# Loading through both DMA queues at the start of an RMSNorm-GELU kernel

## Chip, cores, metric

One core of one Trainium2 chip. The metric is the device time of one execution in microseconds (us). Runs of the kernel before spread by 0.3 to 0.9 us within a job; medians and extremes are given where a difference is that small.

## The reference

x is 8 x 1024 x 2048 float32 (67.1 MB), and so is the result:

```python
rms = np.sqrt(np.mean(x ** 2, axis=-1, keepdims=True) + eps)
out = gamma * x / rms
return 0.5 * out * (1 + np.tanh(np.sqrt(2 / np.pi) * (out + 0.044715 * out ** 3)))
```

## The kernel before

The 8192 rows are 16 groups of 512 rows: 128 partitions with 4 rows (32,768 contiguous bytes) each, 4 MB a group. Six slots hold groups in on-chip memory, and a slot is loaded again when its group has been stored. ScalarE sums squares, GpSimd makes the reciprocal root, VectorE multiplies by gamma (spread over the partitions by four matmuls into PSUM), and ScalarE does GELU with the root as its scale. SyncE issues the loads (queue q1). ScalarE issues gamma's loads and the stores (queue q10).

```python
P, ROWS, SLOTS, GW, CHUNK, NARROW = 128, 4, 6, 32, 512, 128
# ... (pools, tiles: slot[6] is [128, 4, 2048]; gamma_row is [1, D // GW, GW + 4])
    store_pieces = {
        0: [(R, [(0, NARROW), (NARROW, R * D)])],          # group 0: a 64 KB piece first
        G - 1: [(1, [(r * D, r * D + D)]) for r in range(R)],
    }
    def load(g):
        nc.sync.dma_start(out=slot[g % SLOTS], in_=x3[g])
# ... (squares, scale, inverse_rms, gelu_store: whole groups; the last one row by row)
    with tc.manual_schedule():
        for k in range(0, D, CHUNK):                       # gamma: four pieces
            nc.scalar.dma_start(
                out=gamma_row[:, k // GW : (k + CHUNK) // GW, 0:GW],
                in_=gamma[k : k + CHUNK].rearrange("(o a b) -> o a b", o=1, b=GW),
            )
        for g in range(SLOTS):
            load(g)
# ... (constants, four matmuls)
        for g in range(G + 1):
            if g < G:
                squares(g); inverse_rms(g); scale(g)
            if g:
                gelu_store(g - 1)
                if g - 1 + SLOTS < G:
                    load(g - 1 + SLOTS)
```

## Time and profile before

| | before |
|---|---|
| time, median of 3 | 317.31 us (317.09 to 317.42) |
| span of the profiled execution | 315.5 us |
| bytes moved by DMA | 134.25 MB |
| rate from 50 to 270 us | 433 GB/s |

The span is about 1.8 us less than the time. The rate row matters most: the DMA engines are at one fixed rate nearly all the time, so the kernel's length is bytes over rate, plus the places where the engines do less. The lines that show this stand in the prediction.

The trace records each DMA packet; a packet here is one partition's contiguous run. A 32,768-byte one takes 1.213 us at full rate, and the large ones are nearly in proportion (8,192 bytes: 0.309 us for 0.303). **Stall** means what packets of over 4,000 bytes took beyond that (less 12 ns for each, so that rounding is left out), summed over the packets that start in a stretch of time and divided by the 16 engines. The records don't name a packet's engine, so a stall is a mean over the engines.

### The profile page before, as it was taken

The page shows a single profiled execution, that of the slowest core. Times are in us where ns is not written, and L with a number is a line of the kernel's source. Part 1 is how long each engine was busy: PE and PEld are TensorE (multiplying, and loading weights), DVE is VectorE, ACT ScalarE, POOL GpSimd, SP SyncE. Part 2 cuts the span into 40 slices and gives each one's busy share as a digit, 9 for nine tenths or more (in the row PEclk, how much of TensorE's full clock was granted, in tenths as well). Part 3 has the DMA queues.
Part 4 walks back from the last instruction along what each step waited for, and adds up shares of the span by engine and source line. Part 5 has one row for each costly group of instructions (what it writes and reads, how often), then busy time and mean ns, then how long its engine had stood idle before and what let it go on. Part 6 is the DMA issues. An engine that isn't in the chain of part 4 may idle for free.

```text
span 315.5 us, 479 instructions
## 1 busy us (share of the span) xinstructions
PE 7.9 (3%) x8; PEld 2.1 (1%) x8; DVE 139.4 (44%) x21; ACT 251.2 (80%) x194; POOL 32.3 (10%) x101
## 2 busy tenths in 40 slices
PE   0810000000000000000000000000000000000000
PEld 0200000000000000000000000000000000000000
DVE  0028909091918282827328082370824609480000
ACT  1289999999999999989596895969959599598500
POOL 0020202020202020202020020200202002020000
DMA  8999999999999999999999999999999999999997
GB/s 329 404 461 403 459 413 396 453 406 462 403 461 407 457 407 458 411 453 416 449 428 440 432 432 432 432 440 424 446 416 453 411 453 411 453 415 449 416 418 314
DMA packets 5315, 134.25 MB, mean 426 GB/s; under 512 B 704, under 2 KB 832, under 8 KB 832
## 3 DMA queue, kind: packets, MB, share of 16 engines
q1 hardware_dynamic: 2304, 67.11, 49.7%
q10 hardware_dynamic: 3008, 67.12, 49.4%
q14 instruction: 3, 0.02, 0.0%
HBM read 67.12 MB, written 67.11 MB: 425 GB/s over the span
## 4 chain that ended last, share of the span: by engine, by line
ACT 38%; DMA 32%; another core or an unknown queue 18%; issue 5%; ACTq 1%; SPq 0%
ACT slot L111 21%; DMA slot<-in_x_dram 16%; ACT junk L73 16%; DMA out_dram<-slot 15%; ACTq L119 1%; SPq L69 0%; ACTq L111 0%; ACTq L73 0%
## 5 line engine op out<-in xcount | busy, mean ns | idle before, releaser
L83 DVE TENSOR_TENSOR slot<-slot,gamma_ps 128x8192 f32<-128x8192 f32 (+1 forms) x19 | 139.2, 7338 | 142.3 <-ACT junk L73 142.3
L73 ACT ACTIVATE junk<-slot 128x2048 f32<-128x2048 f32 x64 | 120.4, 1881 | 40.8 <-DMA slot<-in_x_dram 36.8
L111 ACT ACTIVATE slot<-slot,rstd 128x2048 f32<-128x2048 f32 x64 | 123.0, 1987 | 1.7 <-ACT slot L111 1.7
L93 POOL TENSOR_SCALAR ms<-ssq 128x4 f32<-128x4 f32 x16 | 3.1, 194 | 242.8 <-ACT junk L73 242.8
L97 POOL TENSOR_TENSOR y<-ms,power 128x4 f32<-128x4 f32 x16 | 16.1, 1009 | 1.3
L73 ACT ACTIVATION_READ_ACCUMULATOR junk<-slot 128x1 f32 x64 | 11.9, 186 | 0.0
L134 PE MATMUL gamma_ps<-gamma_row,ones 1*128 1x512 f32 x8 | 7.9, 1112 | 9.2 <-DMA gamma_row<-in_gamma_dram 9.2
L132 ACT ACT_TABLE_LOAD x1 | 1.3, 1283 | 3.3 <-issue 3.3
L99 POOL TENSOR_TENSOR z<-z,ms 128x4 f32<-128x4 f32 x16 | 3.2, 201 | 1.3
L103 POOL TENSOR_TENSOR rstd<-z,y 128x4 f32<-128x4 f32 x16 | 3.2, 200 | 1.3
L98 POOL TENSOR_TENSOR z<-y 128x4 f32<-128x4 f32 x16 | 3.2, 200 | 1.3
L100 POOL TENSOR_SCALAR z<-z 128x4 f32<-128x4 f32 x16 | 3.1, 195 | 1.4
L134 PEld LDWEIGHTS gamma_ps<-gamma_row,ones 1*128 1x128 f32 x8 | 2.1, 306 | 13.4 <-issue 8.7
L130 DVE MEMSET warm<- 1x1 f32 x1 | 0.1, 59 | 0.8 <-PEq L166 0.8
L132 ACT ACTIVATE warm<-warm 1x1 f32<-1x1 f32 x1 | 0.2, 203 | 0.0
L131 DVE MEMSET ones<- 1x128 f32 x1 | 0.2, 165 | 0.0
L129 POOL MEMSET power<- 128x4 f32 x1 | 0.1, 102 | 0.3 <-POOLq L166 0.3
L166 POOL MEMSET const-float32-0.0<- 128x1 f32 x1 | 0.1, 99 | 0.2 <-issue 0.2
L166 POOL MEMSET const-bfloat16-1.0<- 128x1 bf16 x1 | 0.1, 102 | 0.0
L166 POOL MEMSET const-uint8-127<- 128x1 uint8 x1 | 0.1, 102 | 0.0
L166 POOL MEMSET const-float32-1.0<- 128x1 f32 x1 | 0.1, 99 | 0.0
## 6 DMA issues: line engine op xcount, KB each, us to landing
slot<-in_x_dram SPq DMA_DIRECT2D x16, 4096.0 KB, 29.9
out_dram<-slot ACTq DMA_DIRECT2D x14, 4096.0 KB, 43.3
out_dram<-slot ACTq DMA_DIRECT2D x4, 1024.0 KB, 17.5
out_dram<-slot ACTq DMA_DIRECT2D x1, 4032.0 KB, 28.5
gamma_row<-in_gamma_dram ACTq DMA_DIRECT2D x4, 2.0 KB, 10.3
out_dram<-slot ACTq DMA_DIRECT2D x1, 64.0 KB, 14.4
```

What stands on the lines that cost most here:

```text
L73: nc.scalar.activation(out=junk, in_=slot[g % SLOTS][:, r, :], func=ACT.Square, accum_out=ssq[:, g, r : r + 1],)
L83: nc.vector.tensor_tensor(out=rows, in0=rows, in1=gamma_ps.unsqueeze(1).to_broadcast([P, n, D]), op=ALU.mult,)
L93: v.tensor_scalar(out=ms, in0=ssq[:, g, :], scalar1=1.0 / D, scalar2=eps_f, op0=ALU.mult, op1=ALU.add,)
L97: v.tensor_tensor(out=y, in0=ms, in1=power, op=ALU.pow)
L98: v.tensor_tensor(out=z, in0=y, in1=y, op=ALU.mult)
L99: v.tensor_tensor(out=z, in0=z, in1=ms, op=ALU.mult)
L100: v.tensor_scalar(out=z, in0=z, scalar1=-0.5, scalar2=1.5, op0=ALU.mult, op1=ALU.add)
L103: v.tensor_tensor(out=rstd[:, g, :], in0=z, in1=y, op=ALU.mult)
L111: nc.scalar.activation(out=slot[g % SLOTS][:, r, :], in_=slot[g % SLOTS][:, r, :], func=ACT.Gelu_apprx_tanh, scale=rstd[:, g, r : r + 1],)
L119: nc.scalar.dma_start(out=dst[:, a:b], in_=flat[:, a:b])
L132: nc.scalar.activation(out=warm, in_=warm, func=ACT.Gelu_apprx_tanh)
L134: nc.tensor.matmul(out=gamma_ps[:, k : k + CHUNK], lhsT=ones, rhs=gamma_row[:, k // GW : (k + CHUNK) // GW, 0:GW], start=True, stop=True,)
```

## The change

Its intent: let both queues load at first, so that loads are through early, and let ScalarE's queue pass from its last load to its first store without a gap, so that the small first store piece is not needed.

```diff
-GW = 32
-CHUNK = 512
-NARROW = 128
+HALF = 2
+GW = 64
+GAMMA = [(0, 1024), (1024, 1536), (1536, 2048)]
...
-    gamma_row = sbuf.tile([1, D // GW, GW + 4], FP32, name="gamma_row")
+    gamma_row = sbuf.tile([1, D // GW, GW + 8], FP32, name="gamma_row")
...   (load, store, squares, scale, gelu take a range of rows now; no small store piece)
+        load(nc.sync, 0, 0, HALF)
+        for a, b in GAMMA:
+            nc.scalar.dma_start(
+                out=gamma_row[:, a // GW : b // GW, 0:GW],
+                in_=gamma[a:b].rearrange("(o a b) -> o a b", o=1, b=GW),
+            )
-        for g in range(SLOTS):
-            load(g)
+        load(nc.scalar, 0, HALF, R - HALF)
+        load(nc.sync, 1)
+        load(nc.scalar, 2)
+        load(nc.scalar, 3, 0, 1)
+        load(nc.sync, 3, 1, R - 1)
+        load(nc.sync, 4)
+        load(nc.sync, 5)
...
+        squares(0, 0, HALF)
+        for g in range(G):
+            squares(g, HALF, R - HALF)
+            inverse_rms(g)
+            step = 1 if g in (0, G - 1) else HALF
+            for r in range(0, R, step):
+                scale(g, r, step)
+            if 0 < g < G - 1:
+                squares(g + 1, 0, HALF)
+            if g < G - 1:
+                gelu(g, 0, R)
+                store(g)
+                if g == 0:
+                    squares(1, 0, HALF)
+            else:                      # last group: gelu and store row by row, as before
...
+            if g + SLOTS < G:
+                load(nc.sync, g + SLOTS)
```

More of the change, by code (lines that the diff above doesn't have):

```diff
@@ L58, with load, store, squares @@
     junk = psum.tile([P, D], FP32, name="junk")
-    whole = [(R, [(0, R * D)])]
-    store_pieces = {
-        0: [(R, [(0, NARROW), (NARROW, R * D)])],
-        G - 1: [(1, [(r * D, r * D + D)]) for r in range(R)],
-    }
-    scale_pieces = {G - 1: [(0, 1), (1, 1), (2, 1), (3, 1)]}
-    def load(g):
-        nc.sync.dma_start(out=slot[g % SLOTS], in_=x3[g])
-    def squares(g):
-        for r in range(R):
+    def load(queue, g, r=0, n=R):
+        queue.dma_start(
+            out=slot[g % SLOTS][:, r : r + n, :], in_=x3[g, :, r : r + n, :]
+        )
+    def store(g, r=0, n=R):
+        nc.scalar.dma_start(
+            out=o3[g, :, r : r + n, :], in_=slot[g % SLOTS][:, r : r + n, :]
+        )
+    def squares(g, r, n):
+        for q in range(r, r + n):
             nc.scalar.activation(
                 out=junk,
-                in_=slot[g % SLOTS][:, r, :],
+                in_=slot[g % SLOTS][:, q, :],
                 func=ACT.Square,
-                accum_out=ssq[:, g, r : r + 1],
+                accum_out=ssq[:, g, q : q + 1],
             )
-    def scale(g):
-        for r, n in scale_pieces.get(g, [(0, R)]):
-            rows = slot[g % SLOTS][:, r : r + n, :]
-            nc.vector.tensor_tensor(
-                out=rows,
-                in0=rows,
-                in1=gamma_ps.unsqueeze(1).to_broadcast([P, n, D]),
-                op=ALU.mult,
-            )
+    def scale(g, r, n):
+        rows = slot[g % SLOTS][:, r : r + n, :]
+        nc.vector.tensor_tensor(
+            out=rows,
+            in0=rows,
+            in1=gamma_ps.unsqueeze(1).to_broadcast([P, n, D]),
+            op=ALU.mult,
+        )
     def inverse_rms(g):
@@ L103, in inverse_rms, with gelu @@
         v.tensor_tensor(out=rstd[:, g, :], in0=z, in1=y, op=ALU.mult)
-    def gelu_store(g):
-        flat = slot[g % SLOTS].rearrange("p r d -> p (r d)")
-        dst = o3[g].rearrange("p r d -> p (r d)")
-        row = 0
-        for n, stores in store_pieces.get(g, whole):
-            for r in range(row, row + n):
-                nc.scalar.activation(
-                    out=slot[g % SLOTS][:, r, :],
-                    in_=slot[g % SLOTS][:, r, :],
-                    func=ACT.Gelu_apprx_tanh,
-                    scale=rstd[:, g, r : r + 1],
-                )
-            row += n
-            for a, b in stores:
-                nc.scalar.dma_start(out=dst[:, a:b], in_=flat[:, a:b])
+    def gelu(g, r, n):
+        for q in range(r, r + n):
+            nc.scalar.activation(
+                out=slot[g % SLOTS][:, q, :],
+                in_=slot[g % SLOTS][:, q, :],
+                func=ACT.Gelu_apprx_tanh,
+                scale=rstd[:, g, q : q + 1],
+            )
     with tc.manual_schedule():
-        for k in range(0, D, CHUNK):
+        load(nc.sync, 0, 0, HALF)
+        for a, b in GAMMA:
             nc.scalar.dma_start(
-                out=gamma_row[:, k // GW : (k + CHUNK) // GW, 0:GW],
-                in_=gamma[k : k + CHUNK].rearrange("(o a b) -> o a b", o=1, b=GW),
-            )
-        for g in range(SLOTS):
-            load(g)
+                out=gamma_row[:, a // GW : b // GW, 0:GW],
+                in_=gamma[a:b].rearrange("(o a b) -> o a b", o=1, b=GW),
+            )
+        load(nc.scalar, 0, HALF, R - HALF)
[5 more added lines that the diff above has]
+        load(nc.sync, 5)
         nc.gpsimd.memset(power, -0.5)
@@ L132 @@
         nc.scalar.activation(out=warm, in_=warm, func=ACT.Gelu_apprx_tanh)
-        for k in range(0, D, CHUNK):
+        for k in range(0, D, 512):
             nc.tensor.matmul(
-                out=gamma_ps[:, k : k + CHUNK],
+                out=gamma_ps[:, k : k + 512],
                 lhsT=ones,
-                rhs=gamma_row[:, k // GW : (k + CHUNK) // GW, 0:GW],
+                rhs=gamma_row[:, k // GW : (k + 512) // GW, 0:GW],
                 start=True,
@@ L140 @@
             )
-        for g in range(G + 1):
-            if g < G:
-                squares(g)
-                inverse_rms(g)
-                scale(g)
-            if g:
-                gelu_store(g - 1)
-                if g - 1 + SLOTS < G:
-                    load(g - 1 + SLOTS)
+        squares(0, 0, HALF)
[13 more added lines that the diff above has]
+            else:
+                for r in range(R):
+                    gelu(g, r, 1)
+                    store(g, r, 1)
+            if g + SLOTS < G:
+                load(nc.sync, g + SLOTS)
 _INS = ['x', 'gamma', 'eps']
```

## The prediction

> **What bounds the kernel now.** I read the page's summary first, then stretches of time with their DMA rate, then the waits of the load queue, then the packet records of the two DMA queues.
>
> ```profile
> span 315.5 us, 479 instructions
> PE 7.9 (3%) x8; PEld 2.1 (1%) x8; DVE 139.4 (44%) x21; ACT 251.2 (80%) x194; POOL 32.3 (10%) x101
> DMA  8999999999999999999999999999999999999997
> q1 hardware_dynamic: 2304, 67.11, 49.7%
> q10 hardware_dynamic: 3008, 67.12, 49.4%
> HBM read 67.12 MB, written 67.11 MB: 425 GB/s over the span
> ```
>
> ScalarE, the busiest engine, is idle for a fifth of the span. The DMA row is at nine tenths in all slices but the first and last, and the two queues (q1: SyncE's loads; q10: ScalarE's stores and gamma) take 99.1% of the 16 engines' time. The chain that ended last names ScalarE first (38%), but it runs along an engine that itself waits for loads, in 10 of the 16 groups:
>
> ```profile
> ACT junk L73 <- DMA slot<-in_x_dram: 36.8, 10, 8.7
> ```
> ```profile
> SPq L69 <- DMA out_dram<-slot: 224.3, 10, 53.7
> ```
>
> ScalarE waits 36.8 us for loads; the load queue waits 224.3 us for stores that free a slot. Both are waits on the same DMA engines. The question is therefore only where those engines run below their rate:
>
> ```profile
> 0.00:4.00 4.00, 0.00 (x0) 0.00 (x0) 0.22 (x2) 0.73 (x1) 0.29 (x5) 1.00 0.73 238
> 4.00:44.00 40.00, 7.89 (x8) 2.10 (x8) 17.37 (x2) 29.14 (x27) 4.01 (x12) 1.00 1.00 429
> 44.00:50.00 6.00, 0.00 (x0) 0.00 (x0) 2.71 (x1) 5.97 (x6) 2.00 (x6) 1.00 1.02 393
> 50.00:270.00 220.00, 0.00 (x0) 0.00 (x0) 110.22 (x13) 191.76 (x147) 23.98 (x72) 1.00 1.00 433
> 304.00:315.50 11.50, 0.00 (x0) 0.00 (x0) 0.00 (x0) 0.00 (x0) 0.00 (x0) 1.00 0.82 348
> ```
>
> Last column GB/s. It is 433 over the 220 us in the middle, whatever the mix of loads and stores, and lower in three places: the start, 44 to 50 us, and the last slice. (A packet is counted where it starts, so a short stretch is rough.)
>
> The packet records say it per engine. A full load packet is one partition's 32,768 bytes and takes 1.213 us; the 134.22 MB of x and out are 256 such packets for each of 16 engines, 310.5 us. The first packets start at 1.73 to 2.61 us. Summing what 32,768-byte packets took over 1.213 us, per engine, I find 0.71 us in the first packet, 0.68 us between 44 and 52 us, and under 0.09 us in all the rest. The last packet ends at 314.3: about 2.1 for the start, 310.5, 0.7, 0.7, and some 0.3 for small packets. So of the span only about 5 us is not full-rate transfer. This bounds any gain of a change that moves the same bytes.
>
> The stretch at 44 to 50 us is where the first store begins: a 64 KB piece (128 columns) issued at 33.1 us, whose packets alternate with loads, then the other 4,032 KB, whose first packet starts at 46.76 us. From the moment the small piece's completion is written (45.12 us on the first engine) load packets take 1.4 to 2.0 us. When the next store follows on a running store queue (completions at 65.2 to 67.0 us), every packet takes 1.213 us. The stall is thus a cost of starting the store stream once, not of each store.
>
> **The Trainium skill.** "DMA: Bandwidth & Descriptors", section "Issuing engines are not separate DMA queues", says that transfers started from different engines run on the same 16 DMA engines and interleave, so that a second issuer saves only issue time. The trace agrees: q1 alone moves 433 GB/s at 16 to 34 us, q1 and q10 together 433 later. Section "Where 436 GB/s comes from" gives 435 GB/s as the ceiling of the on-chip fabric; 433 is measured, so two loading queues have no bandwidth to win. Section "Queues, rings and completion order" says that an engine takes turns between its queues packet by packet. The trace agrees: while the 512-byte store packets ran, each followed one 1.213 us load packet. That rule I use below to place the loads.
>
> **The change, part by part.**
>
> *Bytes and small packets.* The same 134.22 MB. A 512-byte packet took 27 ns where the full rate gives 19, so a packet costs some 8 ns beyond its bytes. Group 0 in halves adds 8 packets per engine, group 3 in two parts 8, the small store's removal takes 8 away, gamma goes from four pieces to three: under +0.1 us, and I enter +0.05.
>
> *Order of loads (estimate by taking turns).* SyncE's half of group 0 (16 KB packets) starts as before near 1.7 us. ScalarE issues three gamma pieces first, 0.61 us each in the trace, then its half. Before, the first gamma packet started only at 6.10 us, after four load packets per engine; those are now half as long, so gamma and then the half come in from about 5 to 10 us. SyncE's half lands near 8 us; the other half then alternates with group 1's 32 KB packets (0.61 + 1.21 us, eight times, 14.6 us) and lands at 20 to 24 us, as does group 1. Before, all of group 0 landed at 13.4 and group 1 at 23.0. Group 2 and three quarters of group 3 alternate next ((1.21 + 0.91) x 8 = 17 us, to about 41), then group 3's single row beside group 4 ((0.30 + 1.21) x 8 = 12 us, to about 53).
>
> *First store.* After the second half at 20 to 24: two squares (2.03 us each), 2.3 for the chain on POOL (one row of it in the trace: 21.66 to 24.07), four GELUs of 1.91: store 0 is issued at 34 to 39 us. VectorE's row pieces (2.28 us each in the old last group) mostly lie beside this. Before it was 38.8. At that time ScalarE's queue still holds loads until about 53, so store 0 does follow them directly. Store 1 is ready some 20 us later (59), store 0 lands near 72: from here ScalarE (about 16 us a group) stays ahead of the engines (8.39 MB at 433, 19.4 us a group).
>
> *What it removes from the path.* If the stall belongs to starting a queue, or to the small piece's completion, it goes: -0.68 us. The earlier gamma and the finer pieces on ScalarE and VectorE are beside the transfers and worth nothing. The start stays: the first packet of SyncE is issued at the same moment. Issue time saved: none on the path.
>
> *Slack at the end.* Before:
>
> ```profile
> 271.61 1.88 ACT L73 ACTIVATE junk<-slot 128x2048 f32<-128x2048 f32 x1 [3.68 <-DMA slot<-in_x_dram]
> ...
> 295.02 2.00 ACT L111 ACTIVATE slot<-slot,rstd 128x2048 f32<-128x2048 f32 x1 [0.42 <-ACT slot L111]
> 297.05 0.34 ACTq L119 DMA_DIRECT2D out_dram<-slot  x1
> ```
>
> The last load's data are used at 271.6, the last row is issued at 297.1, and the stores drain until 314.3: 17 us of backlog, of which one 1 MB row needs 2.4. After, the last load is issued when store 9 lands. Stores land 19.4 us apart from about 72, so near 246; it finds its queue nearly empty and needs 20 to 22 us. The landing, about 267, is no later than before, and the new order adds only about 2 us behind it (two squares come ahead of group 14's GELUs). The backlog stays over 10 us: the end is still set by transfers.
>
> Sum: 317.31 + 0.05 - 0.68 = 316.7 if the stall goes, 317.4 if it stays. I give the first 0.65: 316.9; I set 316.8, as an end some tenths lower is possible if the first stall overlaps the second queue's.
>
> **The rivals.** *The stall is that of the first writes to HBM, not of the queue.* Then it moves to about 53 us and the time is 317.4. For it: reads began with a stall of the same size (0.71), and 512-byte writes had been trickling too thinly to count. Against it: those writes ran from 36 us and did not slow a load, and the slow packets begin at that piece's completion. *The stall grows without the small piece in front,* which looks like an earlier cure: up to 0.7 more, 318.0. *ScalarE's half of group 0 comes so late that store 0 misses the end of the loads.* It would have to be 14 us later than I worked out; SyncE's queue would still hold group 5, so even then only the stall returns, 317.4. *The end becomes compute:* the last load would have to land after about 280; then each further us counts. Nothing speaks for it but the early delay of group 0. *Two loading queues move more:* against the measured 433 with one and with two, no.
>
> **Range and chances.** The two main outcomes are 316.7 and 317.4; runs of the old kernel spread by 0.33 us; the start stall may move by some tenths with 16 KB packets. So 316.2 to 317.7. Two per cent is 6.3 us, more than all time not at full rate (about 5 us), so faster by 2% has 0.01. Slower by 2% needs a compute-bound end or idle queues that nothing above shows: 0.02.
>
> **What would show it.** Right: rate 433 from about 5 us to the end with no dip near 53; store 0 issued at 34 to 39, long before its first packet; group 0's second half in at 20 to 24 us; last store issued at 290 to 300. Wrong: a dip where the first store starts (rival 1 or 2), a load queue and a store queue both empty in the middle, or the final stretch with DMA idle before the last row.

## The result, and the profile after

| | before | after |
|---|---|---|
| time, median of 4 each | 317.28 us (317.09 to 317.42) | 318.11 us (317.86 to 318.32) |
| ratio of fast runs, 95% interval | | 1.0026 (1.0009 to 1.0043) |
| span of the profiled execution | 315.5 us | 316.5 us |
| stall in the first packets (0 to 10 us) | 0.69 us | 0.73 us |
| stall where the first store begins | 0.66 us, at 45 to 49 us | 0.71 us, at 48 to 53 us |
| stall after that, to 284 us | 0.04 us | 0.82 us, nearly all at 84 to 88 us |
| the last store's 16 completions | 313.6 to 314.6 us | 314.0 to 315.7 us |

A ratio is the mean time of one kernel's fast runs over that of the other's of the same rounds, so it is not quite the ratio of the medians. The change is within 2%, and it is slower by about 0.8 us. In this job no run of one kernel overlaps one of the other; in the next they do (a_repeat below).

The page of the changed kernel, with the rows that answer to those of before:

```profile
span 316.5 us, 524 instructions
PE 7.2 (2%) x8; PEld 2.5 (1%) x8; DVE 141.0 (45%) x38; ACT 251.3 (79%) x194; POOL 32.1 (10%) x101
DMA  8999999999999999999999999999999999999997
q10 hardware_dynamic: 3232, 74.46, 54.6%
q1 hardware_dynamic: 2160, 59.77, 44.5%
HBM read 67.12 MB, written 67.11 MB: 424 GB/s over the span
```

The work of the engines is the same, and the DMA row has no hole. 7.3 MB of loads have moved from q1 to q10. The waits (who, for whom; us in total, times, longest), first ScalarE's and then the load queue's:

```profile
ACT junk L73 <- DMA slot<-in_x_dram: 27.6, 7, 10.5
```
```profile
SPq L62 <- DMA out_dram<-slot: 229.7, 10, 61.9
```

ScalarE waits 9 us less for loads than before (27.6 against 36.8), and the end comes later all the same: these waits were not what bounded the kernel. The rate by stretches, changed kernel first, then the same late stretch before:

```profile
4.00:48.00 44.00, 7.16 (x8) 2.48 (x8) 14.31 (x6) 26.45 (x23) 3.13 (x8) 1.00 1.01 433
48.00:54.00 6.00, 0.00 (x0) 0.00 (x0) 6.00 (x2) 5.97 (x6) 0.86 (x5) 1.00 0.98 369
54.00:84.00 30.00, 0.00 (x0) 0.00 (x0) 15.58 (x5) 28.97 (x24) 3.98 (x12) 1.00 1.01 436
84.00:90.00 6.00, 0.00 (x0) 0.00 (x0) 3.67 (x1) 6.00 (x4) 0.00 (x0) 1.00 1.01 382
90.00:270.00 180.00, 0.00 (x0) 0.00 (x0) 88.93 (x21) 160.31 (x125) 20.79 (x62) 1.00 1.00 433
```
```profile
84.00:90.00 6.00, 0.00 (x0) 0.00 (x0) 4.15 (x1) 5.55 (x5) 0.00 (x0) 1.00 1.01 437
```

The last column shows two dips where there was one: 369 GB/s where the first store begins, and 382 at 84 to 90 us, where the kernel before had 437. The column before it, the DMA share, stays near 1 in both dips: the engines count as busy, but single load packets take up to 2.6 us in place of 1.213. A busy share does not show this; the rate does.

The end was not bound by compute. In order of time on ScalarE, the last row:

```profile
298.04 2.00 ACT L106 ACTIVATE slot<-slot,rstd 128x2048 f32<-128x2048 f32 x1 [0.42 <-ACT slot L106]
300.07 0.34 ACTq L67 DMA_DIRECT2D out_dram<-slot  x1
```

The last store is issued at 300.07 us and the stores drain until 315.7.

The two profiled executions differ by 1.08 us (318.32 and 317.24); their last packets end at 315.38 and 314.30. The mean of the last store's 16 completions moved by 0.99 us (313.90 to 314.89). The new dip accounts for about 0.8 of this, the other two stalls for under 0.1. The slowest engine now ends 1.7 us after the first, in place of 1.0, but against the mean it lost only 0.1.

### The profile page after: what moved, and what is told of

Read it like the earlier page. It is cut to its first block, busy times and chain, and to the rows that moved or that the text cites. A ratio compares the mean times of both kernels' runs of the same rounds, so it can differ in the third digit from the quotient of the medians.

```text
span 316.5 us, 524 instructions
## 1 busy us (share of the span) xinstructions
PE 7.2 (2%) x8; PEld 2.5 (1%) x8; DVE 141.0 (45%) x38; ACT 251.3 (79%) x194; POOL 32.1 (10%) x101
## 3 DMA queue, kind: packets, MB, share of 16 engines
q10 hardware_dynamic: 3232, 74.46, 54.6%
## 4 chain that ended last, share of the span: by engine, by line
ACT 31%; DMA 30%; another core or an unknown queue 18%; issue 12%; ACTq 2%; POOL 1%; SPq 0%; POOLq 0%
ACT slot L106 20%; DMA slot<-in_x_dram 15%; DMA out_dram<-slot 15%; ACT junk L73 11%; ACTq L67 1%; ACTq L116 1%; POOL y L96 1%; SPq L62 0%; POOL z L98 0%; POOL z L97 0%; POOL ms L92 0%; POOL z L99 0%; POOLq L189 0%; POOL rstd L102 0%
## 5 line engine op out<-in xcount | busy, mean ns | idle before, releaser
L82 DVE TENSOR_TENSOR slot<-slot,gamma_ps 128x4096 f32<-128x4096 f32 (+1 forms) x36 | 140.8, 3944 | 148.9 <-ACT junk L73 135.6
L73 ACT ACTIVATE junk<-slot 128x2048 f32<-128x2048 f32 x64 | 120.4, 1881 | 35.2 <-DMA slot<-in_x_dram 27.6
L132 PE MATMUL gamma_ps<-gamma_row,ones 1*128 1x512 f32 x8 | 7.2, 1072 | 7.0 <-DMA gamma_row<-in_gamma_dram 7.0
## 6 DMA issues: line engine op xcount, KB each, us to landing
slot<-in_x_dram SPq DMA_DIRECT2D x13, 4096.0 KB, 27.6
```

Source lines behind the costliest of these rows:

```text
L73: nc.scalar.activation(out=junk, in_=slot[g % SLOTS][:, q, :], func=ACT.Square, accum_out=ssq[:, g, q : q + 1],)
L82: nc.vector.tensor_tensor(out=rows, in0=rows, in1=gamma_ps.unsqueeze(1).to_broadcast([P, n, D]), op=ALU.mult,)
L132: nc.tensor.matmul(out=gamma_ps[:, k : k + 512], lhsT=ones, rhs=gamma_row[:, k // GW : (k + 512) // GW, 0:GW], start=True, stop=True,)
```

## Experiments

Names that begin with a_ are edits of the changed kernel, b_ of the kernel before. Each job timed the kernel before on the same chip: its medians were 317.33 to 317.55. The jobs ran on different chips (the first three on one, the fourth and the fifth on two others), and the unedited changed kernel ran in the first alone, besides the run of the result, so kernels of different jobs are compared by their ratio to the kernel before. "Later stall" is what comes after the stall at the first store, up to 284 us.

| run | time, us | at the first store | later stall | last store's completions |
|---|---|---|---|---|
| a_repeat | 318.05 (317.57 to 318.13) | 0.71 | 0.38 | 313.7 to 314.9 |
| a_reversed | 318.21 (318.02 to 318.43) | 0.68 | 0.92 | 314.2 to 315.5 |
| b_no_small | 317.44 (317.14 to 317.55) | 0.61 | 0.13 | 313.5 to 314.9 |
| a_g3_sync | 323.51 (322.60 to 324.51) | 0.78 | 3.41 | 314.5 to 320.2 |
| a_halves | 323.03 (321.95 to 323.60) | 0.83 | 2.28 | 314.8 to 319.7 |
| a_small | 317.78 (317.16 to 318.33) | 0.53 | 0.51 | 313.8 to 315.0 |
| a_loads_sync | 322.67 (322.56 to 323.07) | 0.94 | 0.06 | 319.7 to 319.9 |
| b_load_gap | 320.92 (318.82 to 321.74) | 0.65 | 4.03 | 317.0 to 319.0 |
| a_half_row | 318.12 (317.83 to 318.30) | 0.86 | 0.37 | 313.7 to 315.7 |
| b_two_queues | 317.46 (317.34 to 317.59) | 0.48 | 0.11 | 313.3 to 314.8 |
| a_gamma_even | 317.22 (317.19 to 317.72) | 0.59 | 0.07 | 313.6 to 314.7 |
| b_two_queues_g8 | 317.51 (317.16 to 317.81) | 1.00 | 0.04 | 313.8 to 314.9 |
| a_even_plus8 | 318.70 (317.81 to 321.32) | 0.67 | 0.97 | 313.7 to 316.7 |
| a_even_plus16 | 317.81 (317.61 to 317.99) | 0.67 | 0.20 | 313.6 to 314.8 |
| a_gamma_even2 | 317.40 (317.19 to 317.69) | 0.49 | 0.07 | 313.4 to 314.6 |
| a_early_store | 317.56 (317.35 to 317.66) | 0.50 | 0.07 | 313.7 to 314.6 |

All outputs are right.

### First job: does it repeat, and what does it follow?

**a_repeat**: no edit.

> The changed kernel once more, for a second profile of it. If the two stalls of its load packets (0.71 us per engine at 48 to 52 us, 0.73 us at 84 to 88 us, over 1.213 us a packet) belong to the program, both come again within 2 us of the same place and the time is 318.0 +- 0.3. If the second was an accident of that one profiled execution, it is gone from this profile, and the other runs' times (all 0.6 us or more above the kernel before) need another cause.

Both stalls came again at the same places. The second was smaller (0.30 us at 84 to 90 us), and this profiled execution was the fastest of its four, 317.57. So the second dip belongs to the program, but its size varies from one execution to the next. The ratio to the kernel before was 1.0014 (0.9999 to 1.0029): this job alone does not show the changed kernel to be slower.

**b_no_small**, one line out of the kernel before:

```diff
-        0: [(R, [(0, NARROW), (NARROW, R * D)])],
```

> The kernel before without the small first piece of store 0 (one 4 MB store as for the other groups). Theory A (the stall at 45 to 49 us is that of starting bulk stores, whatever goes ahead): still one stall of about 0.7 us, starting when store 0's first packets start (some 5 us after its issue, so at 42 to 46 us); time 317.0 to 317.5. Theory B (the small piece is what the changed kernel lacks, and its absence costs the second stall): a second stall of about 0.7 us later on, time 317.8 to 318.2.

One stall of 0.61 us, at 40 to 43 us, where the whole store 0 now starts; time as before. Theory B falls for this kernel: the small piece neither keeps a stall away nor costs anything.

**a_g3_sync**:

```diff
-        load(nc.scalar, 3, 0, 1)
-        load(nc.sync, 3, 1, R - 1)
+        load(nc.sync, 3)
```

> The changed kernel with all of group 3 on SyncE's queue, so that the queue still has loads left when store 0 lands. Theory C (the second stall follows from the load queue running empty at 72 us and starting again at 76): the queue does not run empty, the second stall is gone, one stall of 0.7 us stays, time 317.2 to 317.6. Theory B (absence of the small piece) or D (address): two stalls remain, time about 318.

Neither theory had this. The load queue did not run empty and the dip at 84 us went, but from 68 us on store packets were slow all along, 3.0 us per engine in sum. Stretches of this kernel:

```profile
50.00:68.00 18.00, 0.00 (x0) 0.00 (x0) 10.91 (x4) 17.48 (x15) 1.99 (x6) 1.00 1.01 437
68.00:90.00 22.00, 0.00 (x0) 0.00 (x0) 12.55 (x3) 21.49 (x16) 2.00 (x6) 1.00 0.99 416
90.00:270.00 180.00, 0.00 (x0) 0.00 (x0) 87.82 (x20) 153.14 (x120) 19.95 (x60) 1.00 1.01 426
```

426 GB/s over 180 us in place of 433, by moving 1 MB of one load to the other queue. Engines also drift apart: a load's 16 completions are 3.2 us apart at 120 us and 7.0 at 280. The rate of a mix of loads and stores is thus not fixed. What sets it is not shown.

**a_reversed**:

```diff
-            out=slot[g % SLOTS][:, r : r + n, :], in_=x3[g, :, r : r + n, :]
+            out=slot[g % SLOTS][:, r : r + n, :], in_=x3[G - 1 - g, :, r : r + n, :]
```

(and the same for the store's o3)

> The changed kernel with the groups' places in x and out reversed (group g works on rows of group 15 - g; result the same). Theory D (a stall is the first touch of some stretch of memory by a store or load): a stall moves to another time or vanishes, as other addresses come first; time changes by one stall, 0.7 us. Theories A and C (order of transfers alone): the same two stalls at the same times, 318.0 +- 0.3.

The same two stalls at the same times. Theory D falls: the stalls go with the order of transfers, not with addresses first touched.

### Second job: is it the load queue that runs empty?

In the changed kernel load 5 is through at about 74 us, and load 6, which had to wait for store 0 (landed 72.1 us), brings its first packets near 76. For these few us only stores run. In the kernel before this does not happen.

**a_halves**:

```diff
-                gelu(g, 0, R)
-                store(g)
+                if g == 0:
+                    gelu(g, 0, HALF)
+                    store(g, 0, HALF)
+                    gelu(g, HALF, R - HALF)
+                    store(g, HALF, R - HALF)
+                else:
+                    gelu(g, 0, R)
+                    store(g)
...
+            if g == 0:
+                load(nc.sync, SLOTS, 0, HALF)
+                load(nc.sync, SLOTS, HALF, R - HALF)
```

> The changed kernel with store 0 in two halves, and load 6 in two halves, the first of which needs only the first half-store: SyncE's queue gets its next load some 10 us earlier (about 62 us) and does not run empty at 72 us; the early loads stay as they are. Theory C (the second stall, at 84 to 88 us, follows from the load queue running empty and starting again): the second stall is gone, the first (0.7 us per engine, where store 0 starts) stays, time 317.2 to 317.6. Theory B or one of the whole mix: two stalls stay, 318.0 +- 0.3. A third way, seen in the run with group 3 on SyncE: stores slow down all along (loads and stores in step), 319 or more.

The edit missed its aim: the first half-store landed only at 66.9 us, and the load queue was empty from 67 to 70 us all the same. Stalls of loads and of stores came repeatedly, the largest 0.9 us at 100 to 108 us, and the time, 323.03, is that of the third way that I had named (319 or more). It says nothing for or against theory C.

**a_small**: store 0 as 128 columns and then the rest, as in the kernel before.

```diff
-                store(g)
+                if g == 0:
+                    nc.scalar.dma_start(out=dst[:, 0:128], in_=flat[:, 0:128])
+                    nc.scalar.dma_start(out=dst[:, 128:], in_=flat[:, 128:])
+                else:
+                    store(g)
```

> The changed kernel with the small first piece of store 0 put back (128 columns, then the rest). Theory B (the small piece keeps the second stall away): one stall, time 317.2 to 317.6. Theory C: the load queue still runs empty near 72 us, two stalls, 318.0 +- 0.3.

317.78, with runs from 317.16 to 318.33, and 0.45 us of stall at 80 to 90 us: the second stall stays. B falls here too.

**a_loads_sync**:

```diff
-        load(nc.scalar, 0, HALF, R - HALF)
+        load(nc.sync, 0, HALF, R - HALF)
...
-        load(nc.scalar, 2)
-        load(nc.scalar, 3, 0, 1)
-        load(nc.sync, 3, 1, R - 1)
+        load(nc.sync, 2)
+        load(nc.sync, 3)
```

> The changed kernel with every load on SyncE's queue, in the order 0 (two halves), 1, 2, 3, 4, 5: the change without its two loading queues; gamma in three pieces, finer steps on ScalarE and VectorE and no small store piece stay. Theory C: group 0's store is issued at 30 to 34 us and finds an empty store queue, the load queue never runs empty, one stall of 0.7 us, time 317.1 to 317.6. If the new order of ScalarE's or VectorE's work costs the time, 318.

The stalls were as theory C has them (one, then nothing), but the time was 5 us over what I expected, for a reason that I had dismissed for the changed kernel: a compute-bound end. Store 0 was issued at 27.4 us, so stores took their half of the engines early, and the last load landed at 287.0 us (272.1 in the changed kernel, 271.6 before). ScalarE's last steps in this kernel:

```profile
287.12 1.88 ACT L73 ACTIVATE junk<-slot 128x2048 f32<-128x2048 f32 x1 [3.27 <-DMA slot<-in_x_dram]
...
312.95 2.00 ACT L106 ACTIVATE slot<-slot,rstd 128x2048 f32<-128x2048 f32 x1 [0.42 <-ACT slot L106]
314.98 0.34 ACTq L67 DMA_DIRECT2D out_dram<-slot  x1
```
and its DMA rows, in 40 slices of 8.0 us:
```profile
DMA  7999999999999999999999999999999999996788
GB/s 297 460 421 392 445 405 449 433 417 455 421 433 441 417 449 425 426 449 421 437 445 417 445 425 425 449 421 437 441 422 441 429 421 449 429 429 275 327 376 343
```

The last four slices are the loss: no backlog of stores is left while the last group is computed, and the last row, issued at 315.0, lands at 319.9. In the changed kernel the two loading queues hold the first store back until most early loads are through. Undone alone, this costs 4.6 us against the changed kernel.

One more thing stands in this trace. The 16 completions of each store lie 3 us apart from the first store (50.8 to 53.8 us) to 189 us, and the later stall is 0.06 us: engines that are 3 us out of step do not by themselves make load packets slow.

**b_load_gap**:

```diff
+    late = sbuf.tile([16, 1], FP32, name="late")
...
                 inverse_rms(g)
+                if g == 3:
+                    nc.sync.dma_start(out=late, in_=rstd[0:16, 3, 0:1])
+                    load(6)
+                    load(7)
```

(and these two no longer at their old places)

> The kernel before with loads 6 and 7 held back on SyncE's queue until the reciprocal roots of group 3 are there (a copy of 16 numbers ahead of them waits for those, near 80 us): the load queue runs empty at 78 us for 3 to 5 us, as in the changed kernel at 72. The store queue has work all the time. Theory C: a second stall of 0.3 to 0.9 us per engine in load packets within some 15 us of the restart, time 317.7 to 318.3. If an empty load queue is harmless: one stall as before, 317.3 to 317.5.

The queue was empty from 78 to 79.7 us. The time, 320.92, is far above either outcome that I had named, because after that came not one stall but one in each second group: 0.66 us at 100 to 110, 0.79 at 140, 0.73 at 180, 0.57 at 220, 0.49 at 260. One of them by stretches:

```profile
98.00:102.00 4.00, 0.00 (x0) 0.00 (x0) 4.00 (x1) 4.00 (x3) 0.00 (x0) 1.00 1.03 426
102.00:107.00 5.00, 0.00 (x0) 0.00 (x0) 2.14 (x1) 4.55 (x4) 0.00 (x0) 1.00 0.97 374
```

These stalls lie where a store ends and the next one begins: of the 4.03 us of later stall, 3.9 are in packets within 1.3 us of a store's completion record, where only a third of the packets are. So a kernel without any of the change can be brought into such stalls by a shift of a few us in its load queue. This favoured theory C at the time; the next job took it back.

### Third job: both queues alone, and another place for the shift

**a_half_row**:

```diff
-        load(nc.scalar, 3, 0, 1)
-        load(nc.sync, 3, 1, R - 1)
+        nc.scalar.dma_start(out=flat[:, 0:1024], in_=src[:, 0:1024])
+        nc.sync.dma_start(out=flat[:, 1024:], in_=src[:, 1024:])
```

> The changed kernel with half a row less of group 3 (512 KB) on ScalarE's queue and that half row on SyncE's: half the step of the run that moved the whole row. Store 0 should land near 68 us and load 5 end near 78 us: the load queue does not run empty, and loads change some 10 us after stores do, as in the kernel before (77.5 and 67.3). Theory C, in its second form (an empty and restarted load queue, as in all six profiles with a second load stall and in none of the four without): no second stall, no slow stores, one stall of 0.7 us, time 317.2 to 317.6, the same as before. If a second stall or slow stores come all the same, the two loading queues themselves (or the order of ScalarE's work) cost it: 318 or more.

My estimate of the times was wrong: store 0 still landed at 72.1 us and load 5 was through at 73.0, so the queue ran empty as before. Time as in the changed kernel. The later stall is only 0.37 us in the mean, but the engines end 2.0 us apart, and the slowest counts.

**b_two_queues**: the kernel before with the split loads.

```diff
-        for g in range(SLOTS):
-            load(g)
+        part(nc.scalar, 0, 2, 2)          # SyncE's half comes ahead of gamma
+        load(1)
+        part(nc.scalar, 2, 0, R)
+        part(nc.scalar, 3, 0, 1)
+        part(nc.sync, 3, 1, 3)
+        load(4)
+        load(5)
```

> The kernel before with the two loading queues alone: group 0 and 3 split and group 2 on ScalarE's queue as in the change; gamma in four pieces, ScalarE's and VectorE's order, and the small store piece stay as before. Theory C: store 0 lands no earlier than in the changed kernel (72 us) and load 5 ends near 74, so the load queue runs empty, a second stall comes within 30 us of the restart, time 317.8 to 318.5. If the changed order on ScalarE and VectorE makes the second stall: one stall, 317.2 to 317.6.

Theory C falls. The load queue was empty from 62 to 75.5 us, longer than in any other run, and no second stall followed (0.05 us at 80 to 90 us); the time is that of the kernel before. Two loading queues by themselves cost nothing and bring nothing.

What then differs? The trace's semaphore updates give the moments at which each of the 16 engines finished its share of a load. For the single row of group 3, the last load on ScalarE's queue, in us:

```
changed kernel   49.2 49.5 50.3 50.4 50.4 50.5 50.5 50.6 | 53.4 53.5 53.5 53.6 53.7 53.7 53.8 53.9
b_two_queues     55.1 55.1 55.2 55.2 55.2 55.2 55.3 55.3   55.3 55.3 55.4 55.4 55.4 55.4 55.5 55.7
```

In the changed kernel eight engines are 3 us ahead of the other eight. The Trainium skill, "DMA: Bandwidth & Descriptors", section "Why a DMA increments its semaphore by 16 and not by 1", says that a DMA uses the largest number of engines up to 16 that divides the slowest dimension of both sides. Gamma's pieces of 512 numbers are now 8 runs of 64, so 8 engines. The trace agrees: there are 32 packets of 256 bytes (in the kernel before, 64 of 128 bytes), and the semaphores of the two small pieces get 9 updates for them in place of 16. Since small packets take turns with large load packets (as the 512-byte ones do in the kernel before), eight engines should begin ScalarE's half of group 0 later than the rest; this is inferred, as the records don't name the engine. That half landed at 20.0 to 21.4 us on eight engines and at 23.3 to 23.8 on the rest.

### Fourth job: gamma's pieces

**a_gamma_even**: the same three pieces, in runs of 32 numbers, so that all use 16 engines.

```diff
-GW = 64
+GW = 32
```

> The changed kernel with gamma in the same three pieces, but each cut into runs of 32 numbers instead of 64, so that the two 512-number pieces are 16 runs and use all 16 DMA engines, not 8. One number is edited. Theory E: in the changed kernel 8 engines have up to four small gamma packets more on ScalarE's queue than the other 8, so their half of group 0 begins some 3 us later; the halves stay out of step (group 3's row lands at 49.2 to 50.6 us on 8 engines, 53.4 to 53.9 on the other 8), and stores and loads then meet differently: second stall. With even gamma all engines land that row within 1 us, the second stall is under 0.15 us though SyncE's queue still runs empty near 72 us, time 317.2 to 317.6. If the engines' step does not matter: second stall of 0.3 us or more, 317.9 to 318.3.

As theory E says: all engines finish group 3's row within 0.7 us (53.9 to 54.6), the dip at 84 us is gone, and the time is 317.22, ratio 0.9995 (0.9983 to 1.0008) to the kernel before. The load queue still ran empty, from 69.4 to 75.8 us. The late stretch of this kernel:

```profile
84.00:90.00 6.00, 0.00 (x0) 0.00 (x0) 4.65 (x2) 6.00 (x4) 0.00 (x0) 1.00 1.01 437
90.00:270.00 180.00, 0.00 (x0) 0.00 (x0) 91.10 (x21) 161.42 (x126) 21.98 (x66) 1.00 1.00 434
```

437 GB/s, as in the kernel before, where the changed kernel had 382. One number in the source takes the second stall away. What it is worth in time is less exact, since the changed kernel did not run in this job: the medians differ by 0.65 to 0.9 us, the ratios to the kernel before (1.0026 and 1.0014 against 0.9995 and, in the repeat below, 1.0000) by 0.4 to 1.0 us. The edit also makes gamma's packets smaller and more, and ScalarE's half of group 0 lands later (24.1 to 24.8 us). Unevenness is thus not the only thing that it changes; the fifth job tries to part them.

**b_two_queues_g8**: b_two_queues with the changed kernel's GW and gamma pieces.

> The reverse: the kernel before with the two loading queues (which alone cost nothing, 317.46) and the changed kernel's gamma pieces, two of which use 8 engines. Theory E: group 3's row lands on the two halves of the engines some 3 us apart, a second stall of 0.2 to 0.8 us comes at 84 to 90 us, time 317.7 to 318.3. If ScalarE's and VectorE's new order is needed for the stall: still 317.3 to 317.6.

The halves were out of step as expected (group 3's row at 49.2 to 50.6 us on seven engines, 52.0 to 53.3 on nine), but no second stall came, and the time is that of the kernel before. Here the stall at the first store was larger (1.00 us), and by 72 us, after stores had run alone, the engines were within 1.0 us of each other again. That does not explain the absence of the second stall: in a_small store 0's completions lie as close (71.2 to 72.0 us), and its second stall came. So uneven gamma is not enough by itself; it needs what else the changed kernel has after it (other order on ScalarE, other time of stores).

### Fifth job: put the unevenness back by other means

**a_even_plus8 and a_even_plus16**: the even kernel with two useless loads behind gamma, in 8 runs of 64 or 16 runs of 32.

```diff
+        for i in range(2):
+            nc.scalar.dma_start(
+                out=spare[i][:, :, 0:64],                                        # or 0:32
+                in_=gamma[0:512].rearrange("(o a b) -> o a b", o=1, b=64),       # or b=32
+            )
         load(nc.scalar, 0, HALF, R - HALF)
```

> The changed kernel with even gamma (317.2) and two useless loads of 512 numbers more on ScalarE's queue behind gamma, each in 8 runs of 64, so that 8 engines carry four small packets more than the other 8 and the halves are out of step again. Theory E (unevenness over the engines makes the second stall): ScalarE's half of group 0 lands on two sets of 8 engines 2 to 4 us apart, a second stall of 0.3 us or more at 84 to 90 us, time 317.8 to 318.3. If only the start time of ScalarE's loads matters: no second stall, 317.2 to 317.6.

> The control: the same two useless loads, each in 16 runs of 32, on all 16 engines. Theory E: all engines stay within 1 us, second stall under 0.15 us, time 317.2 to 317.6, though ScalarE's loads start later still. If their start time matters: second stall or slow stores, 317.8 or more.

With 8 runs, group 3's row landed at 54.0 to 54.2 us on eight engines and at 59.1 to 59.7 on the other eight, 5 us apart where the changed kernel had 3. Stalls came in stores at 75 to 79 us (0.43 us) and in loads at 84 to 91 us (0.35 us). Its four runs lie from 317.81 to 321.32. With 16 runs all engines but one were within 0.4 us (58.9 to 59.2, the last 59.9), and the later stall was 0.20 us. The late stretch, 8 runs first, then 16:

```profile
84.00:90.00 6.00, 0.00 (x0) 0.00 (x0) 6.00 (x2) 5.97 (x6) 1.91 (x6) 1.00 1.03 416
```
```profile
84.00:90.00 6.00, 0.00 (x0) 0.00 (x0) 5.96 (x2) 5.94 (x7) 1.99 (x6) 1.00 1.03 433
```

The two profiles speak for theory E: 0.97 us of later stall against 0.20, and 416 GB/s against 433. But the profiled execution with 8 runs took 319.47 us, one of its two long ones, and in the times the answer is only partial. The two fastest runs with 8 runs (317.81 and 317.92) lie within the range of those with 16 (317.61 to 317.99), and the intervals of the two ratios overlap (1.0013 to 1.0093 and 0.9998 to 1.0025). The kernel with 16 is itself at the time that I had named for the rival, that the start of ScalarE's loads matters (317.8 or more), and 0.4 us above the even kernel of the same job. The two extra loads also put off ScalarE's half of group 0 (it landed at 27.7 to 28.6 us with 16 runs), so the moment at which ScalarE's loads begin may have some weight of its own; this rival is not excluded.

**a_gamma_even2**: the even kernel again, no edit.

> The even kernel once more: 317.2 +- 0.3, second stall under 0.15 us in this profile too, first stall 0.5 to 0.8 us at 50 to 54 us. If the first profile was lucky, a stall of 0.3 us or more at 84 to 90 us.

317.40 us (317.19 to 317.69), ratio 1.0000 (0.9987 to 1.0012). No stall at 80 to 90 us (0.01 us), 0.49 us at the first store. The finding of the fourth job repeats, and the even kernel is equal to the kernel before, not faster.

**a_early_store**: the even kernel, with 64 KB written early into a place of the output that is overwritten later.

```diff
+    early = sbuf.tile([16, 1024], FP32, name="early")
...
+        nc.gpsimd.memset(early, 0.0)
...                                          # behind gamma on ScalarE's queue
+        nc.scalar.dma_start(out=o3[G - 1, 0:16, 0, 0:1024], in_=early)
```

> The even kernel with a store of 16 x 4 KB of zeros into rows that are written again at the end, one packet an engine, on ScalarE's queue behind gamma, so that the first write to memory falls near 6 to 10 us. Theory F (the first stall is that of the first writes to memory): the stall at 50 to 54 us is gone, or moved to about 7 us, where it costs the same unless it overlaps; if it is gone, 316.5 to 316.8. If the stall belongs to bulk stores beginning beside bulk loads: it stays at 50 to 54 us with 0.5 to 0.8 us, time 317.3 to 317.7 (0.15 us for the extra packet).

The early write landed at 12.6 to 13.1 us, and the stall came all the same, 0.50 us at 56 to 58 us, just before store 0's first packets (57.8 us); time 317.56, ratio 1.0004 (0.9990 to 1.0017). So the stall does not belong to the first write of the execution, at least not to a small one. By stretches, this kernel and then the one with all loads on one queue, whose store 0 begins at 32 us:

```profile
48.00:56.00 8.00, 0.00 (x0) 0.00 (x0) 8.00 (x3) 7.94 (x8) 1.99 (x6) 1.00 1.03 434
56.00:60.00 4.00, 0.00 (x0) 0.00 (x0) 2.45 (x1) 4.00 (x3) 0.00 (x0) 1.00 0.98 377
60.00:90.00 30.00, 0.00 (x0) 0.00 (x0) 17.13 (x4) 28.97 (x24) 3.98 (x12) 1.00 1.01 437
```
```profile
24.00:30.00 6.00, 0.00 (x0) 0.00 (x0) 0.00 (x0) 5.54 (x5) 0.00 (x0) 1.00 1.03 437
30.00:34.00 4.00, 0.00 (x0) 0.00 (x0) 2.10 (x1) 3.94 (x5) 0.00 (x0) 1.00 1.03 360
```

One dip each, and it has moved from 30 to 34 us to 56 to 60 with the first full store. In all 18 profiles it sits there, at 0.48 to 1.00 us; the first full store packets start at 43.0 us in b_no_small, 46.8 before, 50.6 after, 61.2 in b_two_queues. The slow packets are nearly all load packets. a_early_store shows them most plainly: there are 16, as many as engines, started at 55.97 to 56.50 us and ended at 57.78 to 58.17, which is when the 16 engines start their first store packets. So the time seems to go in the load packet just before the store's first one.

No version beat the kernel before. The best, a_gamma_even, is at 0.9995 with an interval that holds 1.

## Why the prediction was wrong, point by point

**The bound held.** The rate in the middle is 433 GB/s in both kernels, and the time moved by a quarter of a per cent.

**The placing of the loads held.** SyncE's half of group 0 landed at 7.9 to 9.3 us (near 8 predicted), ScalarE's at 20.0 to 23.8 (20 to 24), the rest of groups 2 and 3 at 38 to 41 (41), the single row at 49.2 to 53.9 (53). Store 0 was issued at 38.2 us (34 to 39), store 1 at 58.4 (59), and store 0 landed at 72.1 (72). Two details were off. The records show three 32,768-byte packets, not four, ahead of the first gamma packet before, and five of half the size after. And the last load, issued at 244.1 us (246), landed at 272.1 and not at 267, because the load ahead of it was still in its queue. There was slack for that: the last row was issued at 300.1 us and the stores drained until 315.7.

**"If the stall belongs to starting a queue, or to the small piece's completion, it goes: -0.68 us"** (given 0.65) failed. Store 0 followed the loads on its queue without a gap and without a small piece, and the stall was 0.71 us. Both named causes are excluded: b_no_small has no small piece and keeps the stall, and the changed kernel has no gap. What the runs put in their place is the beginning of a full store beside running loads, which is what the first rival had named, though its reason, the first writes, is not the cause, at least where a small write stands for them (a_early_store). The dip there was also one of the prediction's own signs of being wrong. That the time came near the second rival's 318.0 is luck: a missing small piece is not what cost it.

**"The stall is thus a cost of starting the store stream once, not of each store"** failed as well. It held in the kernel before, but in the changed kernel the slow load packets at 84.6 to 88.7 us lie where store 1's completions are written (85.8 to 88.7) and store 2's first packets start (from 87.2), and in b_load_gap such stalls came at every second change from one store to the next.

**"gamma goes from four pieces to three: under +0.1 us, and I enter +0.05"** failed too, and it is the term that, in this kernel, goes with the lost time: about 0.8 us where I entered 0.05. I sized gamma by its bytes and packets and did not ask on which engines they run. The packets themselves are cheap, as I said. But two of the pieces have only 8 runs and go over 8 engines, the two halves of the engines are then 3 us apart, and a second stall follows at 84 to 88 us, 0.75 to 0.8 us in the first profile. The sum that was right: 317.3, nothing gained at the first store, about 0.8 from the second stall, 318.1. Shown: the edit of this one number takes the second stall away in three profiles (0.07 us of later stall in a_gamma_even, a_gamma_even2 and a_early_store, against 0.37 to 0.92 in the changed kernel, a_repeat, a_reversed, a_small and a_half_row), and the time returns to that of the kernel before, twice. Argued in part: that it does so through uneven engines. The 8-run loads bring a late stall back and the 16-run loads hardly, in one profile each. Shown as well: it is not sufficient (b_two_queues_g8 and a_loads_sync have engines some 3 us apart and no second stall), nor necessary for such stalls in general (b_load_gap has even gamma and a stall in each second group).

**"The earlier gamma and the finer pieces on ScalarE and VectorE are beside the transfers and worth nothing"** held for the end, but only together with the two queues: with all loads on one queue and the rest of the change kept, the first store comes early, the end becomes bound by compute, and the time is 4.6 us longer.

**What stays open** is the mechanism. Why do load packets take up to about twice their time where one store follows another, why there at 84 us and not at the next such places, and what has unevenness to do with it? Theory B (the small piece), C (an empty load queue), D (addresses) and F (the first write) fell by runs; E (unevenness) is favoured in this kernel, with the limits just told; a start of ScalarE's loads at another time is a rival that stays. What sets 426 GB/s in a_g3_sync for the whole run is not settled either.

## What to carry to other kernels

Try small early loads in a shape that uses all 16 engines: here a change of 64 to 32 in the split of an 8 KB vector was worth about 0.8 us of 318, though the vector's own transfer cost next to nothing. In another arrangement (b_two_queues_g8) the split of 64 cost nothing. A second loading queue brings no bandwidth; it changes when the first store begins and when the last load lands, so look at these two times. Where DMA bounds a kernel, read the rate by stretches and how far apart a transfer's 16 completions are: the busy share stayed near 1 in stretches that moved 369 and 382 in place of 433 GB/s.

## What the Trainium skill lacked or had wrong

- "DMA: Bandwidth & Descriptors", "Why a DMA increments its semaphore by 16 and not by 1": the rule for the number of engines agrees (32 small packets; 9 semaphore updates for a piece of 8 runs in place of 16). What it lacks is a consequence: with small transfers on 8 engines ahead of large ones on the same queue, the large ones landed on two sets of 8 engines 3 us apart, and about 0.8 us was lost that the even split did not lose.
- The same page, "Issuing engines are not separate DMA queues": the bandwidth agrees (433 GB/s with one loading queue or two). That a second issuer only saves issue time held in the kernel before (317.46 us with two loading queues, 317.45 with one) but not in the changed one, which needed 318.11 us with two and 322.67 with one: there the queues also set when the first store begins.
- The same page, "Queues, rings and completion order", says that an engine typically drains 9 to 17 descriptors from a queue before it turns to the next. In the kernel before, at 36 to 45 us, the records show one 512-byte row for each 32,768-byte row.
- No page that I read has these: the first full store beside running loads cost 0.48 to 1.00 us once in each of 18 profiles; a mix of loads and stores ran at 426 in place of 433 GB/s for 180 us (a_g3_sync) or stalled by up to 0.79 us at every second change from one store to the next (b_load_gap).
